# A decoder block with a product-key expert mixer: first-table products in halves between the groups of the gate build, and gate stores issued by ScalarE

## The chip, the cores and the metric

The kernel runs on one core of a Trainium2 chip. The core has five engines that run side by side, each with its own queue of instructions in a fixed order: TensorE (PE, matrix products), VectorE (DVE, elementwise work), ScalarE (ACT, activations and copies), GpSimd (POOL) and SyncE (SP, here only an issuer of transfers). Matrix products write to PSUM, everything else lies in SBUF or in device memory, and transfers (DMAs) move data between the two. The metric is the device time of one execution in microseconds (us). "Start us, us" in a row of the timeline are the start, counted from the first instruction, and the duration.

## The reference

A sequence of 512 tokens with 1024 features goes through one layer: a mixer (state-space heads beside latent attention), a norm, then an expert mixer (PEER), and a norm. Only the expert mixer matters here:

```python
def block(xb):
    q = (xb @ w_query).reshape(T, PEER_HEADS, 2, PEER_HALF_DIM)
    s = jnp.einsum('thkd,hknd->thkn', q, sub_keys)
    sv, si = lax.top_k(s, K)
    ...
    top_s, top_pos = lax.top_k(cand_s, K)
    expert_idx = jnp.take_along_axis(cand_i, top_pos, axis=-1)
    gate = jax.nn.softmax(top_s, axis=-1)
    u = jnp.take(u_table, expert_idx, axis=0)
    act = jax.nn.gelu(jnp.einsum('td,thkd->thk', xb, u), approximate=False)
    v = jnp.take(v_table, expert_idx, axis=0)
    return jnp.einsum('thk,thkd->td', gate * act, v)
```

Each token picks 8 x 16 = 128 of 16384 experts, each an (i, j) pair of 128 x 128 keys. For each one the token's product with a row of the U table goes through a Gelu, is weighted by the gate and multiplies a row of the V table.

## The kernel before

The kernel does not gather these rows for most tokens. For 384 columns (tokens of blocks 0 to 2, of which the last 16 are treated apart, so NU = 368) it multiplies densely with all 16384 experts: 128 *U products* (128 experts each) give Gelu values for all tokens, a *gate matrix* that is zero except for the chosen experts multiplies them, and 128 *V products* accumulate the output. The fourth block of 128 tokens is gathered row by row with indirect transfers during the V phase.

Precision: each fp32 weight tile is split into a high part (`wih`, ScalarE, L109, a copy to a narrower format) and a low part (`wil`, VectorE, L119, the difference), and each product is made of three matmuls (`mm3`, L71): high by high, high by low, low by high. The class `Stream` (L80) does this for all weights in one list of items: `get(n)` issues the low part of item n+2, the high part of item n+3 and the load of item n+5 (`wir`, L91, on SP's queue), so that PE finds its weights ready. `item()` takes the next one.

One U product (`u_chunk`, L1221) takes one item, makes 8 x 3 matmuls into a PSUM tile `pu` (two buffers), fills 16 columns with ones (L1229) and writes the Gelu of the rest to `act` (L1230). 54 of the products (LEAD) are made ahead of the V phase, the others inside it, one beside each V product. Where the 54 are made is decided when the program is written out, by `drive` (L1270): it keeps two counters of estimated time, `tm[0]` for PE and `tm[1]` for VectorE, and lets a step of U (4.07 on the first counter, and 1.2 on the second, for the low part) go before the next piece of VectorE work as long as `tm[0] <= tm[1]`. Up to 43 products fit until a second pool opens, then 52. The pieces come from generators: the index decoding (`stage2`) and then the gate build (`build_g`, L1126).

The gate build has 48 groups of 8 tokens, 16 to a block. For each, VectorE makes one-hot rows from the indices (`hot`: `ij` at L1134, `g` at L1139, one group ahead of PE), PE multiplies them (16 small matmuls, L1157 and L1158, into two `pw` tiles; `pw` has four buffers), and ScalarE copies the result to a staging tile `stg` (L1160, two copies). A staging tile holds four groups. There are two of them, in turn. When one is full, it is stored to device memory in two parts, `gs0` (128 KB, L1164) and `gsp` (1920 KB, L1165), both issued on SP's queue. Two generators put further pieces between the groups: 16 row products (`ug_dots`) in groups 1 to 16, and a few small steps (`ug_head`) in groups 30 to 38. `g_head` transposes the next block's indices on PE (L1115).

Behind the build, `load_g` (L1321) reads the first two pieces of the gate matrix back from `gs0` into `gt` (L1325, SP's queue), the U products still missing from the 54 are made, and the V phase begins: `P` (L1348) is the product of `act` and `gt`, `Ph` and `Pl` (L1361, L1368) are its high and low part, and 18 matmuls (L1377, L1378, L1381) add it to the output accumulators `va`.

Of the kernel before, what the change touches and what calls it, by code (L numbers as in the profile page):

```python
# [17 lines left out]
AF = mybir.ActivationFunctionType  # L18
# [14 lines left out]
NU = NT - UG  # L33
LEAD = 54
KEEP = 43
RES = 2
LASTC = 120
T_U = 4.07
# [15 lines left out]
def tile_block(ctx: ExitStack, tc: tile.TileContext, I, out):  # L54
    nc = tc.nc
    ctx.enter_context(tc.manual_schedule())
    V, A, T, G = nc.vector, nc.scalar, nc.tensor, nc.gpsimd
# [3 lines left out]
    def pool(name, bufs=1, **kw):  # L61
        p = tc.alloc_tile_pool(name=name, bufs=bufs, **kw)
        opened.append(p)
        return p
# [6 lines left out]
    def mm3(ps, lh, ll, rh, rl, start, stop):  # L71
        T.matmul(ps, lh, rh, start=start, stop=False)  # L72
        T.matmul(ps, lh, rl, start=False, stop=False)  # L73
        T.matmul(ps, ll, rh, start=False, stop=stop)  # L74

    def chain(*gs):
        for g in gs:
            yield from g
# [115 lines left out]
    gs0 = dram.tile([NT // 32, 128, 8, 32], F32, name="gs0")  # L194
    gsp = dram.tile([NT // 32, 128, 120, 32], F32, name="gsp")
# [29 lines left out]
    lo_on = [V]  # L225
# [17 lines left out]
    def item():  # L243
        cnt[0] += 1
        return win.get(cnt[0] - 1)
# [86 lines left out]
    def proj(i):  # L332
        if i < 2:
            return two[i]
        hl = item()
        ps = pa()
        for k in range(8):
            proj_k(ps, hl, k)
        return ps
# [226 lines left out]
    for i in range(13):  # L566
        ps = proj(i)
# [63 lines left out]
    for i in range(13, 18):  # L631
        ps = proj(i)
# [13 lines left out]
    for n in range(8):  # L646
# [3 lines left out]
        h, l = item()  # L650
        for kk in range(2):
            k = kp * 2 + kk
# [33 lines left out]
    pu = lambda: psU.tile([128, 512], F32, name="pu")  # L686
# [35 lines left out]
    def v_proj(p):  # L722
        wh, wl = item()
        vh = ml.tile([128, NB, 256], F32R, name="vh", bufs=2)
        vl = ml.tile([128, NB, 256], F32R, name="vl", bufs=2)
        vv[p] = (vh, vl)
        for b2 in range(2):
            ps = pp()
            for e in range(2):
                b = b2 * 2 + e  # L730
                bs = slice(b * 128, (b + 1) * 128)
                for k in range(2):
                    ks = slice(k * 256, k * 256 + 256)
                    mm3(ps[:, e * 256:(e + 1) * 256], kvh[:, k, bs], kvl[:, k, bs], wh[:, ks], wl[:, ks],
                        k == 0, k == 1)
            evac(ps, vh[:, b2 * 2:b2 * 2 + 2].rearrange("p a b -> p (a b)"),
                 vl[:, b2 * 2:b2 * 2 + 2].rearrange("p a b -> p (a b)"))
            yield

    def qk_nope(h):  # L740
        wh, wl = item()
        ps = pp()
        for k in range(3):
            ks = slice(k * 128, k * 128 + 128)
            mm3(ps, wh[:, ks], wl[:, ks], qlh[:, k], qll[:, k], k == 0, k == 2)
        QN[h] = pair("qn")
        A.activation(QN[h][0], ps, AF.Copy, scale=SCALE)
        V.scalar_tensor_tensor(QN[h][1], ps, SCALE, QN[h][0], op0=OP.mult, op1=OP.subtract)
        yield
        ps = pp()  # L750
        for k in range(2):
            ks = slice(384 + k * 128, 512 + k * 128)
            mm3(ps, wh[:, ks], wl[:, ks], kvh[:, k], kvl[:, k], k == 0, k == 1)
        KN[h] = pair("kn")
        evac(ps, *KN[h])
        yield
# [72 lines left out]
    g = chain(qk_nope(1), v_proj(0))  # L829
# [3 lines left out]
    for st in range(39):  # L833
        h, q = divmod(st, 4)
        if q == 0 and h:
            g = iter(())
            if h < 7:
                g = chain(qk_nope(h + 1), v_proj(h // 2)) if h % 2 == 0 else chain(q_pe(h // 2 + 1), qk_nope(h + 1))
# [39 lines left out]
    XTH = xt.tile([128, 8, S], F32R, name="XTH")  # L878
    XTL = xt.tile([128, 8, S], F32R, name="XTL")
    one = xt.tile([128, UG], F32, name="one")  # L880
# [245 lines left out]
    def build_g():  # L1126
        jij = gb.tile([128, 3, 4, 128, 2], F16, name="ij")

        def hot(n):
            ijT, gT = GT[n // 16]  # L1130
            r = n % 2
            col = ijT[:, n % 16 // 2, r].rearrange("p e (q c) -> p (e q) c", c=2)
            b2 = [128, 8, 128, 2]
            V.tensor_tensor(jij[:, 1 - r:3 - r].rearrange("p e q i c -> p (e q) i c"), iotaE[:, None].to_broadcast(b2),  # L1134
                            col[:, :, None, :].to_broadcast(b2), op=OP.is_equal)
            g = gb.tile([128, 2, 4, 128, 2], F16, name="g", bufs=2)
            b4 = [128, 2, 4, 128, 2]
            gv = gT[:, n % 16].rearrange("p e (q c) -> p e q c", c=2)
            V.tensor_tensor(g, jij[:, 1][:, None].to_broadcast(b4), gv[:, :, :, None, :].to_broadcast(b4), op=OP.mult)  # L1139
            return jij[:, 2 - 2 * r], g[:, 0], g[:, 1]  # L1140

        nxt = hot(0)
        dots, head = ug_dots(), ug_head()
        tm[1] += 3.0
        yield 2.6
        for n in range(48):
            b, g = divmod(n, 16)
            oj, oi, g1 = nxt
            if n < 47:
                nxt = hot(n + 1)  # L1150
            if g % 4 == 0:
                stg = gs[n // 4 % 2].tile([128, 128, 32], F32, name="stg")
            for hf in range(2):
                ps = pw()
                for t in range(4):
                    q, c = hf * 2 + t // 2, t % 2
                    T.matmul(ps[:, t * 128:(t + 1) * 128], oj[:, q, :, c], oi[:, q, :, c], start=True, stop=False)  # L1157
                    T.matmul(ps[:, t * 128:(t + 1) * 128], oj[:, q, :, c], g1[:, q, :, c], start=False, stop=True)  # L1158
                q0 = g % 4 * 8 + hf * 4
                A.activation(stg[:, :, q0:q0 + 4],  # L1160
                             ps.rearrange("p (t i) -> p i t", t=4), AF.Copy, scale=1.0 / GSC)
            tm[0] += 1.1
            if g % 4 == 3:
                nc.sync.dma_start(gs0[b * 4 + g // 4], stg[:, 0:8])  # L1164
                nc.sync.dma_start(gsp[b * 4 + g // 4], stg[:, 8:])  # L1165
            if g == 12 and b < 2:
                g_head(b + 1)
            if n >= 1:
                tm[1] += next(dots, 0.0)
            if n in (30, 32, 34, 36, 38):  # L1170
                tm[1] += next(head)
            yield 2.42 if n < 47 else 0.1
# [39 lines left out]
    aps = [pool("act")]  # L1212
    an = [0]
    ACT = {}

    def act_tile():
        k = an[0] % LEAD >= KEEP
        an[0] += 1
        return aps[k].tile([128, NT], F32, name="act", bufs=LEAD - KEEP if k else KEEP)

    def u_chunk(c, psum=None):  # L1221
        h, l = item()
        h = h.rearrange("p (k j) -> p k j", k=8)
        l = l.rearrange("p (k j) -> p k j", k=8)
        ps = (psum or pu)()[:, :NU]
        for k in range(8):
            mm3(ps, h[:, k], l[:, k], XTH[:, k, :NU], XTL[:, k, :NU], k == 0, k == 7)
        ACT[c] = act_tile()
        A.activation(ACT[c][:, NU:], one, AF.Copy)  # L1229
        A.activation(ACT[c][:, :NU], ps, AF.Gelu)  # L1230

    u_chunk(0, pw)
    win.la = 1
# [25 lines left out]
    tm = [0.0, 0.0]  # L1259

    def step_u():
        un[0] += 1
        u_chunk(un[0] - 1)
        tm[0] += T_U
        if lo_on[0] is V:
            tm[1] += 1.2

    un = [uc]

    def drive(fill):  # L1270
        while True:
            if tm[0] <= tm[1] and un[0] < (LEAD - RES if len(aps) > 1 else KEEP):
                step_u()
                continue
            c = next(fill, None)
            if c is None:
                return
            tm[1] += c

    fill = iter(())  # L1280
    for m in range(17):
        if m == 16:
            step_u()
        w_query_fm(m)
        lo_on[0] = G
        tm[0] += T_Q
        if m:
            fill = chain(fill, stage1(m - 1))
            tm[1] = max(tm[1], tm[0] - 3.0)
        while tm[1] < tm[0] + T_Q:  # L1290
            c = next(fill, None)
            if c is None:
                break
            tm[1] += c
# [18 lines left out]
    UR["hd"] = gb.tile([128, UG], F32, name="uhd")  # L1313
    UR["w"] = gb.tile([UG, 128], F32, name="uw")
    UR["m"] = gb.tile([UG, 2], F32, name="um")
    drive(build_g())
    close(gb, *gs)
    vst = pool("vst")
    gt = {}
# [1 line left out]
    def load_g(q):  # L1321
        if q < 32 and q not in gt:
            gt[q] = vst.tile([128, NT // 32, 4, 32], F32, name="gt", bufs=2)
            src, q0 = (gs0, q * 4) if q < 2 else (gsp, q * 4 - 8)
            nc.sync.dma_start(gt[q], src[:, :, q0:q0 + 4, :].rearrange("b j i t -> j b i t"))  # L1325

    for q in range(2):
        load_g(q)
    uc = un[0]
    while uc < LEAD:  # L1330
        u_chunk(uc)
# [118 lines left out]
    fill = gather()  # L1450
# [174 lines left out]
```

## Time and profile before

| | |
|---|---|
| median of three runs | 1623.73 us (1623.13 to 1624.22) |
| profiled execution, its time | 1623.08 us |
| its span, first to last instruction | 1621.3 us |
| PE busy | 1581.0 us, 98% |
| DVE busy | 1357.4 us, 84% |
| ACT busy | 708.1 us, 44% |
| POOL busy | 481.4 us, 30% |
| mean granted TensorE clock | 0.998 |
| first and last copy of the gate build (L1160) | 594.8 and 765.9 us |
| transfers | 395.42 MB, mean 244 GB/s |

Busy shares are averages over stages that have different limits, so the stretch of the gate build, some 590 to 770 us, is read by itself, in windows and in the timelines of single engines. In a row of the timeline, "x1" is the number of instructions merged, and the bracket gives the idle time of the engine before it and what ended it. In a row of a tile or line stand minimum, median and maximum in ns. In a window row each engine's busy time stands with its count of instructions, then the granted clock, the share of the transfer engines that was busy, and GB/s. In the list of waits stand the total in us, the number of times and the longest. PE's matmuls are pipelined: a row's duration is longer than its distance to the next.

### The profile page before, as it was taken

What the parts mean: (1) busy time and instruction counts of PE and PEld (TensorE: products, weight loads), DVE (VectorE), ACT (ScalarE), POOL (GpSimd) and SP (SyncE); (2) the same over time, 40 slices, a digit from 0 to 9 for tenths busy, and PEclk for the clock granted to TensorE, in tenths of its full rate; (3) what the DMA queues carried; (4) which work ended last, traced back from release to release, by engine and by line L of the source; (5) the groups of instructions that cost most, each with busy time, mean ns of one, the idle gap of its engine ahead of it and who ended that gap; (6) DMA issues with size and microseconds to landing.
All of it is one profiled execution on the core that took longest, in us unless ns stands there. A gap on an engine that the chain in (4) does not pass through costs nothing.

```text
span 1621.3 us, 23808 instructions
## 1 busy us (share of the span) xinstructions
PE 1581.0 (98%) x8643; PEld 1393.0 (86%) x8643; DVE 1357.4 (84%) x2564; ACT 708.1 (44%) x1231; POOL 481.4 (30%) x340
## 2 busy tenths in 40 slices
PE   6999999999999999999999999999999999999997
PEld 5777878888888999999999999999999999888886
DVE  8978667747799999998478888888888888889877
ACT  5575467641433445555433433333333333333341
POOL 0000010000133223100035555555555555555300
PEclk9999999999999999999999999999999999999999
DMA  6242122364432459767689999999999999999973
GB/s 243 94 157 91 46 77 57 114 235 143 133 92 81 136 179 344 272 241 255 201 282 360 358 341 342 359 352 343 349 351 350 343 343 360 353 338 362 334 226 118
DMA packets 152253, 395.42 MB, mean 244 GB/s; under 512 B 12776, under 2 KB 65720, under 8 KB 150344
## 3 DMA queue, kind: packets, MB, share of 16 engines
q1 hardware_dynamic: 108408, 238.35, 43.3%
q0 software_dynamic: 43584, 155.29, 26.1%
q8 instruction: 68, 1.11, 0.3%
q14 instruction: 49, 0.40, 0.1%
q10 hardware_dynamic: 144, 0.26, 0.0%
HBM read 359.99 MB, written 31.78 MB: 242 GB/s over the span
## 4 chain that ended last, share of the span: by engine, by line
PE 74%; DVE 18%; ACT 3%; issue 3%; DMA 2%; SPq 0%; DVEq 0%; ACTq 0%
PE va L1377 10%; PE va L1381 10%; PE va L1378 10%; PE pu L72 9%; PE pu L74 8%; PE pu L73 8%; PE pa L74 3%; PE pa L73 3%; PE pa L72 3%; DVE ij L1134 2%; DVE wil L119 2%; DVE t L955 1%; DMA wir<-ut 1%; DVE ti L959 1%; DVE ti L952 1%
## 5 line engine op out<-in xcount | busy, mean ns | idle before, releaser
L109 ACT ACTIVATE wih<-wir 128x1024 fp32r<-128x1024 f32 (+2 forms) x269 | 278.0, 1034 | 275.0 <-DMA wir<-v 94.4
L119 DVE TENSOR_TENSOR wil<-wir,wih 128x1024 fp32r<-128x1024 f32 (+1 forms) x254 | 301.9, 1189 | 98.7 <-ACT wih L109 53.8
L74 PE MATMUL pu<-XTH,wil 128*128 128x368 f32 x1008 | 331.8, 329 | 1.0 <-DVE wil L119 0.9
L72 PE MATMUL pu<-XTH,wih 128*128 128x368 f32 x904 | 299.0, 331 | 1.3 <-ACT act L1230 1.3
L73 PE MATMUL pu<-XTL,wih 128*128 128x368 f32 x904 | 296.9, 328 | 0.0
L1378 PE MATMUL va<-wil,Ph 128*128 128x512 f32 x726 | 282.7, 389 | 0.0
L1415 POOL DMA_INDIRECT row<-u,ix x128 | 190.9, 1491 | 256.7 <-DVE row L1426 126.1
L1415 POOL DMA_INDIRECT row<-v,ix x128 | 193.8, 1514 | 168.5 <-DVE ac L1432 142.9
L74 PEld LDWEIGHTS pu<-XTH,wil 128*128 128x128 f32 x1008 | 189.1, 188 | 1.7 <-DVE wil L119 1.6
L72 PEld LDWEIGHTS pu<-XTH,wih 128*128 128x128 f32 x904 | 169.5, 188 | 4.8 <-ACT act L1230 1.9
L73 PEld LDWEIGHTS pu<-XTL,wih 128*128 128x128 f32 x904 | 169.8, 188 | 2.9
L1377 PE MATMUL va<-wih,Ph 128*128 128x512 f32 x432 | 168.6, 390 | 0.0
L1432 DVE SCALAR_TENSOR_TENSOR ac<-row,hd,ac 128x1024 f32<-128x1024 f32 x128 | 164.0, 1281 | 3.5 <-DMA row<-v,ix 1.2
L1378 PEld LDWEIGHTS va<-wil,Ph 128*128 128x128 f32 x726 | 136.3, 188 | 25.8
L1230 ACT ACTIVATE act<-pu 128x368 f32<-128x368 f32 x126 | 59.9, 476 | 219.5 <-PE pu L74 219.4
L1426 DVE SCALAR_TENSOR_TENSOR row<-row,x 128x1024 f32<-128x1024 f32 x128 | 150.3, 1219 | 3.9 <-DMA row<-u,ix 3.7
L109 ACT ACTIVATE wihx<-wir 128x1024 fp32r<-128x1024 f32 x67 | 71.1, 1061 | 146.1 <-DMA wir<-v 120.5
L1381 PE MATMUL va<-wih,Pl 128*128 128x512 f32 x432 | 133.3, 390 | 0.0
L119 DVE TENSOR_TENSOR wil<-wir,wihx 128x1024 fp32r<-128x1024 f32 x62 | 75.8, 1223 | 51.4 <-issue 36.8
L1377 PE MATMUL va<-wihx,Ph 128*128 128x512 f32 x294 | 114.9, 391 | 0.0
L1381 PEld LDWEIGHTS va<-wih,Pl 128*128 128x128 f32 x432 | 81.0, 188 | 17.2
L1377 PEld LDWEIGHTS va<-wih,Ph 128*128 128x128 f32 x432 | 81.2, 188 | 15.9
(458 smaller groups left out, 3066.3 us busy)
## 6 DMA issues: line engine op xcount, KB each, us to landing
wir<-ut SPq DMA_DIRECT2D x128, 512.0 KB, 5.7
wir<-v SPq DMA_DIRECT2D x128, 512.0 KB, 6.6
gsp<-stg SPq DMA_DIRECT2D x12, 1920.0 KB, 7.4
gt<-gsp SPq DMA_DIRECT2D x30, 768.0 KB, 9.9
wir<-wo SPq DMA_DIRECT2D x26, 512.0 KB, 3.6
wir<-wf SPq DMA_DIRECT2D x18, 512.0 KB, 3.3
wir<-wqr SPq DMA_DIRECT2D x16, 512.0 KB, 3.6
de<-acd POOLq DMA_DIRECT2D x8, 512.0 KB, 5.2
```

Of the source, the lines that this page charges most:

```text
L72: T.matmul(ps, lh, rh, start=start, stop=False)
L73: T.matmul(ps, lh, rl, start=False, stop=False)
L74: T.matmul(ps, ll, rh, start=False, stop=stop)
L109: A.activation(h, r, AF.Copy)
L119: self.lo(n).tensor_tensor(l, r, h, op=OP.subtract)
L1230: A.activation(ACT[c][:, :NU], ps, AF.Gelu)
L1377: T.matmul(va[b][e], Ph[:, bs], h[:, cs], start=c == 0, stop=False)
L1378: T.matmul(va[b][e], Ph[:, bs], l[:, cs], start=False, stop=False)
L1381: T.matmul(va[b][e], Pl[:, bs], h[:, cs], start=False, stop=c == 127)
L1415: G.indirect_dma_start(out=R[s], out_offset=None, in_=I["u"] if s < 128 else I["v"], in_offset=bass.IndirectOffsetOnAxis(ap=ix[:, s % 128: ...
L1426: V.scalar_tensor_tensor(r, r, 1.0, x3, op0=OP.mult, op1=OP.mult, accum_out=hd[:, s:s + 1])
L1432: V.scalar_tensor_tensor(ac, r, hd[:, s - 128:s - 127], ac, op0=OP.mult, op1=OP.add)
```

## The change

A U product is now issued in two halves of 12 matmuls by `u_half`. The first takes the item and the PSUM tile, and the second ends with the two activations. `UO` holds a product of which one half is issued. `drive` counts T_U / 2 for each half and has a second argument: at least that many halves before each further piece. It is 1 for the gate build and 0 elsewhere. A group counts 0.95 in place of 1.1 on the first counter. If a half is pending at the end of the build, its second half follows behind `load_g`. The two stores of a staging tile are issued by ScalarE, in its own queue, in place of SP.

```diff
-            tm[0] += 1.1
+            tm[0] += 0.95
             if g % 4 == 3:
-                nc.sync.dma_start(gs0[b * 4 + g // 4], stg[:, 0:8])
-                nc.sync.dma_start(gsp[b * 4 + g // 4], stg[:, 8:])
+                nc.scalar.dma_start(gs0[b * 4 + g // 4], stg[:, 0:8])
+                nc.scalar.dma_start(gsp[b * 4 + g // 4], stg[:, 8:])
...
+    UO = {}
+
+    def u_half(c, e, psum=None):
+        if e == 0:
+            UO[c] = [z.rearrange("p (k j) -> p k j", k=8) for z in item()] + [(psum or pu)()[:, :NU]]
+        h, l, ps = UO[c]
+        for k in range(4 * e, 4 * e + 4):
+            mm3(ps, h[:, k], l[:, k], XTH[:, k, :NU], XTL[:, k, :NU], k == 0, k == 7)
+        if e:
+            del UO[c]
+            ACT[c] = act_tile()
+            A.activation(ACT[c][:, NU:], one, AF.Copy)
+            A.activation(ACT[c][:, :NU], ps, AF.Gelu)
+
     def u_chunk(c, psum=None):
-        h, l = item()
...
-        A.activation(ACT[c][:, :NU], ps, AF.Gelu)
+        for e in range(2):
+            u_half(c, e, psum)
...
     def step_u():
-        un[0] += 1
-        u_chunk(un[0] - 1)
-        tm[0] += T_U
-        if lo_on[0] is V:
+        e = len(UO)
+        u_half(un[0], e)
+        un[0] += e
+        tm[0] += T_U / 2
+        if not e and lo_on[0] is V:
             tm[1] += 1.2
...
-    def drive(fill):
+    def drive(fill, least=0):
+        n = 0
         while True:
-            if tm[0] <= tm[1] and un[0] < (LEAD - RES if len(aps) > 1 else KEEP):
+            if (tm[0] <= tm[1] or n < least) and un[0] < (LEAD - RES if len(aps) > 1 else KEEP):
                 step_u()
+                n += 1
                 continue
             c = next(fill, None)
             if c is None:
                 return
             tm[1] += c
+            n = 0
...
         if m == 16:
             step_u()
+            step_u()
...
-    drive(build_g())
+    drive(build_g(), 1)
...
     for q in range(2):
         load_g(q)
+    if UO:
+        step_u()
     uc = un[0]
```

More of the change, by code (lines that the diff above doesn't have):

```diff
@@ L1219, in act_tile @@
         return aps[k].tile([128, NT], F32, name="act", bufs=LEAD - KEEP if k else KEEP)
-    def u_chunk(c, psum=None):
-        h, l = item()
[L1223 to L1230, printed above, removed]
+    UO = {}
[10 more added lines that the diff above has]
+            A.activation(ACT[c][:, :NU], ps, AF.Gelu)
+    def u_chunk(c, psum=None):
+        for e in range(2):
+            u_half(c, e, psum)
     u_chunk(0, pw)
```

## The prediction

> **What bounds the kernel now.** I read the page first: busy shares and the slices.
>
> ```profile
> PE 1581.0 (98%) x8643; PEld 1393.0 (86%) x8643; DVE 1357.4 (84%) x2564; ACT 708.1 (44%) x1231; POOL 481.4 (30%) x340
> PEclk9999999999999999999999999999999999999999
> ```
>
> TensorE (PE) bounds the whole at an undisturbed clock, so only its idle time can be won. The second view is the busy time by stages: the stretch that the change touches, and the V phase behind it.
>
> ```profile
> core 0: us, PE busy (x) PEld busy (x) DVE busy (x) ACT busy (x) POOL busy (x), PEclk, DMA share, GB/s
> 590.82:795.74 204.92, 198.12 (x1665) 190.81 (x1665) 178.91 (x179) 110.73 (x218) 23.48 (x16) 1.00 0.74 260
> 795.74:1000.00 204.26, 204.26 (x1058) 185.72 (x1057) 166.57 (x250) 81.10 (x133) 97.71 (x66) 1.00 0.92 324
> 1000.00:1200.00 200.00, 200.00 (x1039) 182.15 (x1038) 168.06 (x242) 74.41 (x123) 111.14 (x75) 1.00 0.96 349
> ```
>
> In the V phase PE is busy in every microsecond. In the first stretch it idles 204.92 - 198.12 = 6.8 us. Its matmul ends are modelled and cover the start of each gap, so I count the idle time a second way, with ScalarE's timeline. The Gelu of a U product (L1230) starts when its 24 matmuls end.
>
> ```profile
> 590.34 0.48 ACT L1230 ACTIVATE act<-pu 128x368 f32<-128x368 f32 x1 [0.68 <-PE pu L74]
> 594.34 0.48 ACT L1230 ACTIVATE act<-pu 128x368 f32<-128x368 f32 x1 [1.66 <-PE pu L74]
> 601.22 0.48 ACT L1230 ACTIVATE act<-pu 128x368 f32<-128x368 f32 x1 [2.38 <-PE pu L74]
> 606.20 0.48 ACT L1230 ACTIVATE act<-pu 128x368 f32<-128x368 f32 x1 [2.38 <-PE pu L74]
> 692.75 0.48 ACT L1230 ACTIVATE act<-pu 128x368 f32<-128x368 f32 x1 [2.39 <-PE pu L74]
> 701.46 0.48 ACT L1230 ACTIVATE act<-pu 128x368 f32<-128x368 f32 x1 [2.39 <-PE pu L74]
> 764.90 0.48 ACT L1230 ACTIVATE act<-pu 128x368 f32<-128x368 f32 x1 [2.38 <-PE pu L74]
> 773.89 0.48 ACT L1230 ACTIVATE act<-pu 128x368 f32<-128x368 f32 x1 [2.47 <-PE pu L74]
> 787.26 0.48 ACT L1230 ACTIVATE act<-pu 128x368 f32<-128x368 f32 x1 [1.91 <-PE pu L74]
> 795.26 0.48 ACT L1230 ACTIVATE act<-pu 128x368 f32<-128x368 f32 x1 [0.44 <-PE pu L74]
> L1230 ACT ACTIVATE act<-pu x38: 457/478/481, 590.3 to 795.3; 128x368 f32<-128x368 f32 x38
> L1115 PE MATMUL px<-ident,ijg 128*128 128x128 f32 x8 | 1.2, 273 | 0.0
> ```
>
> The first two Gelus are U17 and U18 with nothing between: a U costs PE 4.00 us. From 601.22 to 606.20 lie one group and one U: 4.98, so a group costs 0.985 (taken so from several such steps), the changeover on both sides included. From U17 to U54 are 37 U products, all 48 groups and two sets of transposes: 37 x 4.00 + 48 x 0.985 + 1.2 = 196.5 us of work in 795.26 - 590.34 = 204.9. So PE idles **8.4 us** there. It is spread: 601.22 - 594.34 = 6.88 for two groups and one U (5.97), 0.9 idle; 701.46 - 692.75 = 8.71 for three groups and one U (6.96), 1.75 idle, and once more so near 755; 787.26 - 773.89 = 13.37 for three U, 1.37 idle; the rest in bits.
>
> Why it idles in the build is read from VectorE's (DVE) timeline, the first four rows, and from the list of waits (total, times, longest).
>
> ```profile
> 690.02 1.22 DVE L119 TENSOR_TENSOR wil<-wir,wih 128x1024 fp32r<-128x1024 f32 x1
> 691.15 1.22 DVE L1134 TENSOR_TENSOR ij<-iotaE,ijT 128x2048 f16<-128x2048 f16 x1
> 696.32 1.23 DVE L1134 TENSOR_TENSOR ij<-iotaE,ijT 128x2048 f16<-128x2048 f16 x1
> 761.03 1.22 DVE L1139 TENSOR_TENSOR g<-ij,gT 128x2048 f16<-128x2048 f16 x1
> PE pw L1157 <- DVE g L1139: 4.1, 4, 1.5
> ACT wih L109 <- DMA wir<-ut: 8.0, 2, 7.0
> PE pu L72 <- ACT act L1230: 1.1, 1, 1.1
> ```
>
> From 691.15 to 696.32 DVE prepares two groups without a pause: 2.585 each when adjacent; a split (wil) of a U adds 1.13 to 1.14. Where groups come without U between, PE (0.985 a group) starves behind DVE (2.585).
>
> **The change part by part.** *Where the U products go.* I walk the two counters of drive. Before, they place U17 to U47 before the build ends (31), with runs of two or three groups bare, and U48 to U53 behind it. With halves, 0.95 a group, and at least one half before each further group, they give U17 to U49 and the first half of U50: 33.5. No two groups are adjacent any more; groups 0, 1 and 18 on get mostly one half each, a few get two, groups 2 to 7 a whole U as before. All 54 lead products still precede the V phase, so no work is added on PE except changeovers: 48 groups now stand singly, and 48 x 0.985 charges each with both sides already. PE's floor for the stretch stays 196.5 us: the last lead product U53 and U54 end at 590.34 + 196.5 = 786.8 against 795.26.
>
> *Does DVE keep up?* Its last group is ready at 761.03 + 1.22 = 762.25. Before that it did the splits of U17 to U46; in the new order those of U47 to U49 come too: 3 x 1.14 = 3.4, so 765.7, less about 1.0 that it waited for PE before (below nothing it cannot cost: the splits must be done). PE, never idle, would reach group 47 after U18 to U49 and 47 groups: 590.34 + 32 x 4.00 + 47 x 0.985 + 1.2 = 765.8. The two bounds meet. Neither has slack, and each has to wait for the other now and then: group n+2's one-hot writes the buffer that group n's matmuls read. I charge this coupling 0.8 us; its ends are 0 and the 4.1 us that PE waits for g now. Group 47 then ends at 766.6 + 1.0 = 767.6, and U50 to U54 follow, 5 x 4.00: 787.6.
>
> *Halves.* A half keeps its PSUM tile across a group. pu has two buffers and pw four, so no group is refused a tile: nothing. The split, high part and load of a U are issued with its first half, in the old order; the Gelu up to a group (3 us) later; U53's Gelu is needed far later, as the V phase takes products from 0 on: nothing.
>
> *Stores on ScalarE's queue.* The rows are, in this order: issues and copies by tile and by line, the longest work of ScalarE in a U from the page, SP's waits, SP's timeline at the end of the build, three steps of the V phase's start, and the DMA issues with the time to landing.
>
> ```profile
> L1165 SPq DMA_DIRECT2D gsp<-stg x12: 413/426/937, 608.2 to 766.9; - x12
> L1160 ACT ACTIVATE stg<-pw x96: 592/597/622, 594.8 to 765.9; 128x512 f32<-128x512 f32 x96
> L1528 ACTq DMA_DIRECT2D out_dram<-xr x1: 369/369/369, 1617.9 to 1617.9; - x1
> L91 SPq DMA_DIRECT2D wir<-ut x9: 328/332/4300, 742.5 to 797.1; - x9
> L109 ACT ACTIVATE wih<-wir 128x1024 fp32r<-128x1024 f32 (+2 forms) x269 | 278.0, 1034 | 275.0 <-DMA wir<-v 94.4
> SPq L1164 <- ACT stg L1160: 36.0, 12, 4.5
> 766.49 0.33 SPq L1164 DMA_DIRECT2D gs<-stg  x1
> 768.39 3.44 SPq L1325 DMA_DIRECT2D gt<-gs  x2
> 771.89 4.78 SPq L91 DMA_DIRECT2D wir<-ut  x2
> 788.47 0.55 DVE L1348 TENSOR_TENSOR P<-act,gt 128x384 f32<-128x384 f32 x1
> 791.64 0.52 ACT L1361 ACTIVATE Ph<-P 128x384 fp32r<-128x384 f32 x1
> 792.19 0.56 DVE L1368 TENSOR_TENSOR Pl<-P,Ph 128x384 fp32r<-128x384 f32 x1 [3.17 <-ACT Ph L1361]
> gt<-gs SPq DMA_DIRECT2D x2, 768.0 KB, 10.1
> gsp<-stg SPq DMA_DIRECT2D x12, 1920.0 KB, 7.4
> wir<-ut SPq DMA_DIRECT2D x32, 512.0 KB, 3.8
> ```
>
> SP loses 12 pairs of issues and the 36 us that it stood waiting for stg with loads behind it. ScalarE gains 12 x (0.33 + 0.43) = 9 us of issue, behind its own stg copies, so the wait is short. Behind a pair are queued the high part (wih) of a U three ahead, the next Gelu and the next copies. In the late build a block of four groups and two U takes PE at least 4 x 0.985 + 2 x 4.00 = 11.9 us; of that ScalarE works 8 x 0.60 (copies) + 2 x (1.03 + 0.48) = 7.8, so a hold below 4.1 us a block delays nobody. One ACT-queue issue in the trace took 0.37 us; the dearest issue on SP, behind a full queue, 4.3. I take 0.8 a pair, near the first, since ScalarE's queue holds nothing else: nothing on the path. Ends: 0, and 4.3 + 0.3 = 4.6 a pair, which is 0.5 over the slack in each of the eight late blocks: 4 us.
>
> *The stall after the build.* The load at 771.89 stood behind the last stores and two gt loads and held a wih for 7 us, which held U50's Gelu and cost PE the 1.37. In the new order three more U have issued their loads before load_g, and the loads behind load_g belong to items read later, so that goes. The next thing late could be gt: issued when the first store has landed, 768.39 - 766.49 = 1.9 after it, and landing 10.1 later. New: group 47 at 767.6, copies 1.1, so 768.7 + 1.9 + 10.1 = 780.7, and three short steps (P, Ph, Pl, 0.55 + 0.52 + 0.56, with their handovers under 3 us) to the first V matmul: 784 against 787.6. Hidden by 4 us; without that cover each microsecond more is one on the path.
>
> [...]
>
> *Sum.* 787.6 - 795.26 = **-7.7 us**. The V phase is the same program and PE-bound, so it moves whole. I charge 0.4 for anything that catches up there (0 to 2). -7.3 on the profiled execution's 1623.08 (its span 1621.3 and 1.8 around it) is 1615.8; that execution lies 0.65 under the median of the runs, and half of that gives 1616.1.
>
> **The rivals.** *DVE takes the path.* If DVE and PE, both without slack, trip each other more, by the upper end of the coupling (4.1) instead of 0.8, the gain falls to 4.0: about 1619.4. For it: DVE is 179 of 205 us busy in the stretch and gets 3 splits more. Against: the dots end at group 16, and DVE there runs ahead.
>
> *No gain.* The idle time only moves: into the start of the V phase (gt costs from a landing 14 us after its issue on, and all of the gain at 21) or into ScalarE holds. Then 1621 to 1625, taken as 1623.
>
> *Slower: ScalarE is held at the store.* If a store issue blocks ScalarE for longer than 4.1 us a block, copies and Gelus slip, pu's two tiles run out and PE stops. At 6.5 us a block the 8 late blocks lose 8 x 2.4 = 19 us, less 7.3: 1635. It decides from 4.1 + 7.3 / 8 = 5.0 us. For it: the 4.3 us issue on SP. Against: that one came behind 1.9 MB of store and two gt loads on one queue; on ScalarE's queue a store meets nothing of its own.
>
> *Slower: stores land late.* Stores now compete with loads in place of going ahead of them. Block n+2's copies reuse block n's stg. A store needs 7.4 us, two U loads of a block 2 x 3.8: 15.0 at worst, where a block, about 12, is allowed; then 8 x 3 = 24 us of ScalarE wait, of which its slack of 4.1 a block takes all. At 17 us of landing the wait is 5 a block, past the slack by 0.9, and 8 x 0.9 = 7 us takes the gain; at 18.5 it is 6.5 a block and 1635, as above. [...]
>
> **How the numbers follow.** Forecast 0.62 (1614 to 1617.5); DVE on the path 0.14; no gain 0.13; ScalarE held 0.07; stores late 0.04. A difference under 0.2% (3.2 us) can't be told from none: the first two are faster, 0.76; the third the same, 0.13; the last two slower, 0.11. The range begins at PE's floor with nothing charged (8.4 less than 1623.08 is 1614.7) less 1.5 for an overestimated group cost, 1613.2, and reaches past the DVE rival to 1620.9.
>
> **What would show it.** In the changed profile the first V matmul stands at 787 to 788; PE idles some 1 to 2 us from U17 to there; no gap of 1.7 is left between groups; ScalarE's queue shows 24 issues of about 0.4 us. Wrong would be: PE waiting for g by 4 us and more (DVE), P waiting for gt (read-back), or stg copies waiting for a store.

## The result, and the profile after

The changed kernel takes 1617.48 us (median of six runs, 1616.28 to 1619.66) against 1623.97 us (six runs) before: a ratio of 0.9958 with a 95% interval of 0.9948 to 0.9969, so 6.5 us less (5.0 to 8.4). The forecast was 1616.1 in a range of 1613.2 to 1620.9.

The profiled execution took 1618.11 us, its span 1616.4 us. PE's granted clock fell to half for 3.4 us near 265 us in it, far ahead of the changed code. The profile of before has no such fall, and U18's Gelu comes 1.4 us earlier there. So the stretch of the change is compared by itself, from the Gelu of U18 (594.34 us before, 595.71 after) to the first V matmul. The two windows, the first of the kernel before, the second of the changed one:

```profile
594.34:795.10 200.76, 193.96 (x1642) 186.91 (x1640) 174.75 (x175) 109.09 (x214) 23.48 (x16) 1.00 0.75 264
```

```profile
595.71:790.00 194.29, 193.12 (x1641) 185.73 (x1639) 173.52 (x173) 108.41 (x211) 23.54 (x16) 1.00 0.77 271
```

6.5 us went, and by the window PE's idle time fell from 6.80 to 1.17 us. Busy time fell by only 0.8, since no work was taken away. From the first V matmul to the end of the span it is 1621.3 - 795.1 = 826.2 before and 1616.4 - 790.0 = 826.4 after: the V phase moved whole.

Three rows of the list of waits of the changed kernel, over the build (total, times, longest):

```profile
PE pw L1157 <- DVE g L1139: 1.2, 3, 0.5
DVE gT L1123 <- ACT gT L1122: 3.7, 2, 2.2
ACT act L1232 <- issue: 2.2, 1, 2.2
```

The first row is the wait for one-hot rows, down from 4.1. The second was 1.1 before (longest 0.8), and the third is new. Their longest waits belong together, and ScalarE's timeline shows where:

```profile
707.32 1.80 ACTq L1165 DMA_DIRECT2D gsp<-stg  x1
709.16 0.22 ACT L1232 ACTIVATE act<-one 128x16 f32<-128x16 f32 x1 [2.24 <-issue]
709.64 1.08 ACT L1160 ACTIVATE stg<-pw 128x512 f32<-128x512 f32 x2
710.60 0.46 ACT L1121 ACTIVATE ijT<-px 128x128 f16<-128x128 f32 x2
```

One issue of a store took 1.80 us instead of 0.45. Behind it stood the copies of the next block's indices, VectorE waited 2.2 us for them, and then PE for VectorE, 0.4 and 0.5 us at two of the next groups. In the late build two groups and one U now follow each other like this, first two Gelus of the kernel before, then three of the changed one:

```profile
680.52 0.48 ACT L1230 ACTIVATE act<-pu 128x368 f32<-128x368 f32 x1 [2.39 <-PE pu L74]
686.64 0.48 ACT L1230 ACTIVATE act<-pu 128x368 f32<-128x368 f32 x1 [2.39 <-PE pu L74]
```

```profile
739.21 0.48 ACT L1233 ACTIVATE act<-pu 128x368 f32<-128x368 f32 x1 [1.55 <-PE pu L74]
745.21 0.48 ACT L1233 ACTIVATE act<-pu 128x368 f32<-128x368 f32 x1 [1.33 <-PE pu L74]
751.21 0.48 ACT L1233 ACTIVATE act<-pu 128x368 f32<-128x368 f32 x1 [1.33 <-PE pu L74]
```

6.00 us a step, where two adjacent groups and a U took 6.12. The runs of three groups and a U, 8.71 for 6.96 of work, no longer occur.

### The profile page after: what moved, and what is told of

It reads as the page before. It is cut to its first block, busy times and chain, and to the rows that moved or that the text cites. A ratio compares the mean times of both kernels' runs of the same rounds, so it can differ in the third digit from the quotient of the medians.

```text
span 1616.4 us, 23785 instructions
## 1 busy us (share of the span) xinstructions
PE 1581.7 (98%) x8643; PEld 1392.5 (86%) x8643; DVE 1357.5 (84%) x2564; ACT 708.9 (44%) x1231; POOL 479.2 (30%) x340
## 4 chain that ended last, share of the span: by engine, by line
PE 80%; DVE 14%; ACT 3%; DMA 1%; issue 1%; DVEq 0%; ACTq 0%
PE va L1391 10%; PE va L1395 10%; PE va L1392 10%; PE pu L72 10%; PE pu L74 10%; PE pu L73 10%; PE pa L74 3%; PE pa L73 3%; PE pa L72 3%; DVE t L955 1%; PE pw L73 1%; PE pw L74 1%; PE pw L72 1%; PE pw L1157 1%; DVE wil L119 1%; PE pw L1158 1%
## 5 line engine op out<-in xcount | busy, mean ns | idle before, releaser
L119 DVE TENSOR_TENSOR wil<-wir,wih 128x1024 fp32r<-128x1024 f32 (+1 forms) x254 | 302.0, 1190 | 94.0 <-ACT wih L109 54.8
L1429 POOL DMA_INDIRECT row<-v,ix x128 | 189.2, 1478 | 173.1 <-DVE ac L1446 147.8
L119 DVE TENSOR_TENSOR wil<-wir,wihx 128x1024 fp32r<-128x1024 f32 x62 | 75.8, 1223 | 41.3 <-issue 29.9
```

The lines of the kernel that those rows point to most:

```text
L119: self.lo(n).tensor_tensor(l, r, h, op=OP.subtract)
L1429: G.indirect_dma_start(out=R[s], out_offset=None, in_=I["u"] if s < 128 else I["v"], in_offset=bass.IndirectOffsetOnAxis(ap=ix[:, s % 128: ...
```

## The experiments

Theory A: PE idled because VectorE could not supply adjacent groups, and more U products in the build fill that time. Rivals: only their number counts and not the halves (the first form of A), or only the spacing (B); the freed SP queue is what helps (C); adjacent groups wait for something of their own, not for VectorE (D). Each ratio is against the kernel before, run on the same chip in the same set. Times of different sets come from different chips, so a difference between two edited kernels of different sets is also given counted from each set's own kernel before, or by the stretch. The halves with a group still counted 1.1 were not run, so what the counter adds to them stays open.

**The changed kernel again.** No edit.

> The changed kernel again, beside the others of this set: about 6.5 us below before, near 1617.5 (both theories). In its trace U18's Gelu to the first V matmul should take about 194.3 us, as in the first profile (before: 200.8).

Measured: 1617.33 us, ratio 0.9959 (0.9945 to 0.9972). U18's Gelu to the first V matmul: 193.8 us. The long store issue is there again, 1.68 us at the same place, so it is no chance of one execution. All five runs had a mean granted clock of 0.997. In this set the fourteen runs of the kernel before with that clock have a median of 1624.43 us, so at the same clock the gain is 7.1 us.

**The counter alone.**

```diff
-            tm[0] += 1.1
+            tm[0] += 0.95
```

> Only the group's 0.95 on the planner's first counter; U products whole, stores on SP. The counters then place 33 whole U products in the build (before 31, changed kernel 33.5), two groups adjacent between most of them, never three. Theory A (what counts is how many U products lie in the build): the triples (2 x 1.75 us idle) go and the stall behind the build (1.37) goes, the pairs stay at VectorE's 6.12 per two groups instead of 5.97: 3 to 5.5 us gained, near 1619.5. Theory B (what counts is the spacing in halves): the pairs keep starving PE, at most 2 us gained, 1622 or more.

Measured: 1621.75 us, ratio 0.9989 (0.9980 to 0.9998), 2.5 us less: between the two bands. The window of the stretch in this kernel:

```profile
594.21:792.70 198.49, 193.84 (x1641) 186.82 (x1639) 173.46 (x175) 108.51 (x213) 23.54 (x16) 1.00 0.76 267
```

33 U products lie in the build, almost as many as in the changed kernel (33.5), and still it is 4.2 us behind it there. So the number alone gives less than half of the gain, under the 3 to 5.5 us of theory A's first form, and a little more than B allowed. Its pairs run at VectorE's pace:

```profile
690.26 0.48 ACT L1230 ACTIVATE act<-pu 128x368 f32<-128x368 f32 x1 [2.39 <-PE pu L74]
696.39 0.48 ACT L1230 ACTIVATE act<-pu 128x368 f32<-128x368 f32 x1 [2.39 <-PE pu L74]
```

6.13 us a step. Either VectorE is too slow for adjacent groups (A2), or these wait for their own tiles (D).

**The stores alone.**

```diff
-                nc.sync.dma_start(gs0[b * 4 + g // 4], stg[:, 0:8])
-                nc.sync.dma_start(gsp[b * 4 + g // 4], stg[:, 8:])
+                nc.scalar.dma_start(gs0[b * 4 + g // 4], stg[:, 0:8])
+                nc.scalar.dma_start(gsp[b * 4 + g // 4], stg[:, 8:])
```

> Only the two stores moved to ScalarE's queue; U products whole and counted as before. Theory A: PE's waits in the build hang on VectorE and not on a transfer, so 0 to 1.4 us gained (the stall behind the build at most), 1622.5 to 1624. Rival C (the freed SP queue is what helps): 3 us or more gained, below 1621.

Measured: 1624.99 us, ratio 1.0007 (0.9998 to 1.0016). No gain.

```profile
594.06:795.40 201.34, 194.06 (x1641) 186.87 (x1639) 175.03 (x175) 110.22 (x214) 23.53 (x16) 1.00 0.74 264
```

The stretch is no shorter (200.76 before). Rival C falls.

**The halves without the stores.** The changed kernel with the two lines above on SP again.

> The changed kernel with both stores issued by SP again. Theory A: as fast as the changed kernel within 1.5 us, or up to 1.2 us faster, since the one store issue that held ScalarE for 1.8 us ahead of the transposed indices is gone: 1616.3 to 1618. Rival C: it loses 3 us or more of the gain, 1620.5 or more.

Measured: 1617.38 us, ratio 0.9960 (0.9946 to 0.9973).

```profile
595.68:788.80 193.12, 192.83 (x1641) 185.80 (x1639) 172.96 (x172) 107.94 (x211) 23.55 (x16) 1.00 0.77 273
```

As fast as the changed kernel; in its trace 0.7 to 1.2 us shorter in the stretch, the size of the waits behind the long store issue, but the medians don't show it. The whole gain is the halves' and the planner's, none of it the stores'.

**Low parts on GpSimd.** The same edit in three kernels, meant to relieve VectorE: from group 17 to the end of the build the difference of L119 is computed by GpSimd. In the kernel before, in the one with the counter alone, and in the changed one:

```diff
-    win = Stream(..., lo=lambda n: lo_on[0])
+    win = Stream(..., lo=lambda n: G if lo_g else lo_on[0])
...
         for n in range(48):
+            if n == 17:
+                lo_g.append(1)
...
+    lo_g.clear()
     close(gb, *gs)
```

> The kernel before, same order of U products and groups, but from group 17 to the end of the build the low parts (wil) are computed by GpSimd in place of VectorE. Theory A2 (where groups stand adjacent PE waits for VectorE's one-hot rows): VectorE loses 14 x 1.14 = 16 us of work there, pairs go from 6.12 to about 5.95 and triples lose part of their 1.75: 2.5 to 4.5 us faster, near 1620.5. Rival D (adjacent groups wait for something of their own, their PSUM tiles or ScalarE's copies): no change, within 1 us.

> The kernel with 0.95 on the planner's counter alone (whole U products, pairs of groups; 1621.75 by itself), with the low parts from group 17 on by GpSimd. Theory A2: the pairs no longer wait, 15 x 0.15 to 0.2 plus the 1.1 at groups 18 and 19: 3 to 4 us faster than without, near 1618, as fast as halves or nearly. Rival D: 1621 to 1622 as before.

> The changed kernel with the low parts from group 17 on by GpSimd. Theory A2: its late build is at PE's own pace already (5.98 to 6.00 for two groups and a U) and only 1.2 us of waits for VectorE are left, so 0 to 1.5 us faster: 1616 to 1617.3. If VectorE set the pace (the forecast's first rival), more: 1615 or less.

Measured: 1652.92 (ratio 1.0169, 1.0153 to 1.0185), 1646.08 (1.0131, 1.0115 to 1.0148) and 1632.28 us (1.0046, 1.0031 to 1.0060). All three are slower than the kernel before, by 29, 22 and 8 us, against every expectation. Against the same kernels without the edit they lose 29, 24 and 15 us, each counted from the kernel before of its set. In the first two PE's granted clock also fell: to 0.89 from 675 to 770 us in the first, and to 0.989 and 0.990 in the mean of the two profiled executions, where the third had 0.998. So a part of their loss is the clock's. In the third it stayed at 1.00 from 590 to 820 us. VectorE's and GpSimd's timelines in the last one show where the time goes:

```profile
697.93 3.31 DVE L1140 TENSOR_TENSOR g<-ij,gT 128x2048 f16<-128x2048 f16 x1
701.34 1.23 DVE L1135 TENSOR_TENSOR ij<-iotaE,ijT 128x2048 f16<-128x2048 f16 x1
702.60 1.23 DVE L1140 TENSOR_TENSOR g<-ij,gT 128x2048 f16<-128x2048 f16 x1
```

```profile
697.42 2.74 POOL L119 TENSOR_TENSOR wil<-wir,wih 128x1024 fp32r<-128x1024 f32 x1 [4.53 <-PE pu L74]
704.68 2.74 POOL L119 TENSOR_TENSOR wil<-wir,wih 128x1024 fp32r<-128x1024 f32 x1 [4.53 <-PE pu L74]
```

A `g` that starts 0.5 us into GpSimd's subtraction takes 3.31 us instead of 1.23: it ends 1.08 us after GpSimd does, as if it had run only then. VectorE is spared 1.14 us a U and loses 2.08. From 675 to 800 us the 29 `g` took 2.23 us in the mean and the 28 `ij` 1.37, beside 13 subtractions of 2.82. Why a `g` there lasts past GpSimd's end isn't shown. As an experiment on theory A2 these runs don't count as meant. They do show that VectorE's time decides: made longer, it costs PE, which waits 14.3 us for one-hot rows in the third. The kernel with singly placed groups loses least (15 against 29).

**The transposed indices two groups earlier**, in the changed kernel:

```diff
-            if g == 12 and b < 2:
+            if g == 10 and b < 2:
```

> The changed kernel with the transposed indices of the next block made two groups earlier (behind group 10 in place of 12), so that ScalarE's three small copies for them no longer stand right behind a store issue. If the 1.8 us store issue ahead of them is what made VectorE wait 2.2 us and PE 1.2 us, those two waits go: 0.5 to 1.5 us faster than the changed kernel, 1616 to 1617. If it was only a chance of that execution: no difference.

Measured: 1617.28 us, ratio 0.9950 (0.9936 to 0.9964); the changed kernel stood at 1617.33 and 1617.48. The issues of the large store, first in the changed kernel run again, then in this one:

```profile
L1165 ACTq DMA_DIRECT2D gsp<-stg x12: 326/450/1675, 609.2 to 771.2; - x12
```

```profile
L1165 ACTq DMA_DIRECT2D gsp<-stg x12: 356/450/681, 608.6 to 770.0; - x12
```

The long issue is gone, and the stretch took 193.1 us instead of 193.8. The edit moved only the copies, yet the issue itself became short too, so this run doesn't tell the copies' place from the issue's length. What makes that one issue long stays open. The worth of both, under 1 us, can't be told in the times.

**Low parts left out, with the counter alone.** No other engine works beside VectorE here: from group 17 to the end of the build the third matmul of a U takes the high part once more. The kernel leaves out a part of the U products' precision by this and serves as a measurement only.

```diff
-                l = self.tiles(n, 1)[:, :r.shape[-1]]
-                self.lo(n).tensor_tensor(l, r, h, op=OP.subtract)
+                if lo_g:
+                    l = h
+                else:
+                    l = self.tiles(n, 1)[:, :r.shape[-1]]
+                    self.lo(n).tensor_tensor(l, r, h, op=OP.subtract)
```

> The kernel with 0.95 on the planner's counter alone (whole U products, pairs of groups; 1621.75), and from group 17 to the end of the build the low parts are left out: the third matmul takes the high part instead, so PE's work is the same and VectorE has 16 x 1.14 us less, with no other engine working beside it. It leaves out a part of the U products' precision. Theory A2 (adjacent groups wait for VectorE): pairs go from 6.12 to 5.92, so 15 x 0.2 and about 1 us at groups 18 and 19: near 1617.7, as fast as with halves. Rival D (adjacent groups wait for their PSUM tiles, ScalarE's copies or a changeover): 1621 to 1622.

Measured: 1618.74 us, ratio 0.9965 (0.9951 to 0.9979), 3.0 us less than with the low parts (3.5 counted from each set's own kernel before); the stretch is 3.3 us shorter, and its pairs have dropped from 6.13 to 5.93 us:

```profile
595.55:790.70 195.15, 192.31 (x1642) 187.12 (x1640) 157.05 (x159) 107.52 (x213) 23.53 (x16) 1.00 0.75 272
```

```profile
691.19 0.48 ACT L1236 ACTIVATE act<-pu 128x368 f32<-128x368 f32 x1 [2.29 <-PE pu L74]
697.12 0.48 ACT L1236 ACTIVATE act<-pu 128x368 f32<-128x368 f32 x1 [2.33 <-PE pu L74]
```

This is A2: adjacent groups wait for VectorE, and with VectorE relieved they cost PE 5.93, less than two single groups with their changeovers (6.00). Rival D falls.

**Low parts left out, in the changed kernel.** The same edit, and the same part left out.

> The changed kernel with the same low parts left out. Theory A2: PE stands at its own pace already and only some 0.5 to 1.2 us of waits for VectorE can go: 1616 to 1617.3. If VectorE sets the pace in the changed kernel: 1615 or less.

Measured: 1615.08 us, ratio 0.9944 (0.9931 to 0.9958), 2.3 us below the changed kernel (2.7 counted from each set's own kernel before). By the time alone that is next to the rival's band (1615 or less) and below theory A2's. But the clock has a part in it: all five runs had a mean granted clock of 0.998, and the changed kernel 0.997 in all five of its second set; its only run at 0.998 took 1616.28. The trace is free of this:

```profile
594.10:786.70 192.60, 192.60 (x1642) 185.72 (x1640) 155.04 (x157) 109.63 (x213) 23.86 (x16) 1.00 0.77 273
```

The stretch took 192.6 us, 1.2 to 1.7 less than in the changed kernel (193.8 and 194.3), and PE was busy in all of it: 18 us less VectorE work buy 1.2 to 1.7 us. So in the changed kernel VectorE costs PE only its last waits. 192.6 is also PE's floor, measured.

**The large store in twelve pieces**, in the changed kernel, to lengthen ScalarE's hold:

```diff
-                nc.scalar.dma_start(gsp[b * 4 + g // 4], stg[:, 8:])
+                for z in range(8, 128, 10):
+                    nc.scalar.dma_start(gsp[b * 4 + g // 4][:, z - 8:z - 8 + 10], stg[:, z:z + 10])
```

> The changed kernel with each large store of the gate matrix cut in 12 pieces, all issued by ScalarE: 13 issues a block of some 0.35 to 0.45 us, about 5 us, where the forecast counts 4.1 us of slack a block. By the forecast's slack: 8 late blocks x about 1 us, 5 to 11 us slower than the changed kernel, 1622 to 1628. If issues cost ScalarE less than their rows show, or PE's spare tiles take the hold: within 1.5 us of the changed kernel, below 1619.

Measured: 1659.02 us, ratio 1.0215 (1.0201 to 1.0228), 41.7 us more than the changed kernel. The issues cost more than a piece's row of 0.45 suggested:

```profile
692.80 0.33 ACTq L1164 DMA_DIRECT2D gs<-stg  x1
693.16 6.82 ACTq L1166 DMA_DIRECT2D gsp<-stg  x12
700.03 1.06 ACT L109 ACTIVATE wih<-wir 128x1024 fp32r<-128x1024 f32 x1 [7.26 <-DMA gsp<-stg]
```

In this block ScalarE stands for 7.3 us. In the first six blocks, up to 715 us, the two stores hold it for 6.7 to 9.6 us, 8.1 in the mean. The kernel loses 41.7 / 12 = 3.5 us a block, but its mean granted clock was 0.991, against 0.997 in the changed kernel: some 10 us of the loss (an estimate, 0.009 x 1658.6 - 0.003 x 1616.4 of the two spans) are the clock's, which leaves some 32, 2.6 a block. A mean hold of 8.1 less the forecast's slack of 4.1 would be 4.0. So a hold above the slack does cost PE, and the slack was of the right order, if rather too small. With one large store (0.33 + 0.45 us) the hold stays far under it, which fits that the stores cost nothing.

**Without the minimum of one half**, in the changed kernel:

```diff
-    drive(build_g(), 1)
+    drive(build_g())
```

> The changed kernel without the minimum of one half between two groups (halves, 0.95 and ScalarE's stores stay). The counters then leave groups adjacent at 0 and 1, 22 and 23, 24 and 25, 26 and 27, 28 and 29, 33 and 34, with a whole U behind each. Theory A2: some 0.5 us for the first and 0.15 to 0.6 for each other, 1 to 2.5 us slower than the changed kernel: 1618.3 to 1620. If the halves alone do it: as the changed kernel, 1617.4.

Measured: 1620.90 us, ratio 0.9977 (0.9968 to 0.9986): 3.5 us worse than the changed kernel, more than expected.

```profile
596.04:793.40 197.36, 193.52 (x1642) 186.39 (x1640) 174.66 (x175) 109.58 (x213) 23.25 (x16) 1.00 0.75 269
```

```profile
596.04 0.48 ACT L1233 ACTIVATE act<-pu 128x368 f32<-128x368 f32 x1 [1.83 <-PE pu L74]
603.38 0.48 ACT L1233 ACTIVATE act<-pu 128x368 f32<-128x368 f32 x1 [2.36 <-PE pu L74]
779.65 0.48 ACT L1233 ACTIVATE act<-pu 128x368 f32<-128x368 f32 x1 [2.47 <-PE pu L74]
787.68 1.06 ACT L109 ACTIVATE wihx<-wir 128x1024 fp32r<-128x1024 f32 x1 [7.55 <-DMA wir<-v]
788.75 0.46 ACT L1233 ACTIVATE act<-pu 128x368 f32<-128x368 f32 x1
```

The first pair, groups 0 and 1, costs 603.38 - 596.04 - 5.97 = 1.4 us; PE waited for one-hot rows twice in this kernel, 1.3 and 0.6 us. The rest is the stall behind the build, which is back: the high part waits 7.55 us for its load and holds the Gelu behind it, and from U51's Gelu at 779.65 to the first V matmul at 793.4 PE needs three U (12.0) and takes 13.75. The kernel with the counter alone has the same stall (1.7 us). In both the build ends with a whole U, 50 in all; in the changed kernel with the first half of the next, whose step issues one more load ahead of `load_g`.

## Why the prediction was right

*Where PE idles, and why.* Right. PE's floor for the stretch was put at 196.5 us from U17 on, so 192.5 from U18 on; the run without low parts had PE busy in every microsecond of 192.6. That VectorE starves adjacent groups is shown by leaving its low parts out: 6.13 to 5.93 a pair.

*The stretch.* 7.7 us were forecast, 6.5 came in the first profile and 6.9 in the second (200.76 - 193.82). The term that was too small is the coupling of PE and VectorE: 0.8 charged, 1.2 to 1.7 measured above the floor of 192.6. Its cause was not the buffers of the one-hot rows, as the step had it (VectorE waited 0.3 us for PE to free one in the whole build), but mostly the store issue that held ScalarE: with SP's stores 0.5 is left. The median of 1617.48 lies at the upper end of the forecast's own band, 1614 to 1617.5.

*DVE keeps up.* Right: its pace of 6.12 for two groups and a U is slower than PE's 6.00, but with single groups it can use the lead that it gained by group 17. Two low parts of the changed kernel, with two groups between them, show the pace:

```profile
740.57 1.22 DVE L119 TENSOR_TENSOR wil<-wir,wihx 128x1024 fp32r<-128x1024 f32 x1
746.69 1.22 DVE L119 TENSOR_TENSOR wil<-wir,wih 128x1024 fp32r<-128x1024 f32 x1
```

By the two timelines the rows of group 17 are ready 3.2 us before PE uses them, those of group 47 only 0.4 us. The lead lasts just to the end of this build, so a longer one would have run at VectorE's pace (an estimate from these two leads; no run shows it). The first rival (VectorE on the path) is refuted by the run without low parts: 18 us less work gave 1.2 to 1.7.

*Halves cost nothing.* Right: 6.00 a step against the 5.97 counted.

*Stores on ScalarE cost nothing.* In the time, yes: alone (a ratio of 1.0007) and undone (1617.38 us beside the changed kernel's 1617.33) they make no measurable difference. In the trace one issue out of twelve took 1.7 to 1.8 us, where 0.8 for a pair was taken, and it stood ahead of copies on which VectorE waits. The rival "ScalarE is held" is a real mechanism; twelve pieces made it cost 41.7 us, the lower clock included.

*The stall after the build goes.* Right, and for the reason given, loads issued ahead of `load_g`, but closer than the forecast told: three more U were credited. The kernels whose build ends with a whole U have two more U in it than before, and keep 1.7 us or so of the stall; so it hangs on the last half and its one load.

*gt is hidden.* Hidden, but not by 4 us. The read-back was issued 775.4 - 770.8 = 4.6 us after the first store, where 1.9 was counted, since SP waited longer for that store to land, 4.4 us after its issue instead of 1.7:

```profile
SPq L1337 <- DMA gs<-stg: 4.2, 1, 4.2
```

P did not wait for gt, but Ph stood on ScalarE behind a high part that waited 4.9 us for its load, and was ready at 789.5, with the first V matmul at 790.0. PE lost nothing there, with little to spare. In the kernel with halves and SP's stores this row is 0.3 us, in the one with the stores alone 4.4, so the longer landing came with ScalarE's queue.

*The V phase moves whole*, with 0.4 charged: 826.2 to 826.4, so 0.2.

*Stores late.* The large store landed after 7.9 us instead of 7.4 (at most 10.8), the small one after 2.6 instead of 1.7; the 15 of the rival did not occur.

## What to carry to other kernels

Here two engines each had just enough time, and what decided was how evenly the one's work was laid between the deliveries of the other: almost the same number of products gave 2.5 us in whole pieces, and 6.5 in halves with one between any two deliveries. Read the pace of each engine for one step from its own timeline, take the sum of PE's work as the floor, and don't hope for more. Moving transfers to another engine's queue gained nothing here (1.0007), where no wait of PE in the build ended with them, and it put the issues in front of that engine's own work (one of 1.80 us).

## What was unexpected of the hardware

A VectorE instruction beside a GpSimd subtraction took 3.31 us in place of 1.23, and moving 14 or so such subtractions to the idle engine made each kernel 15 to 29 us slower than without.

PE's granted clock fell near 265 us in nine of the fourteen profiles, with halves and with whole U products alike, at two short gaps of PE (1.53 and 0.44 us in the changed kernel). Windows of the changed kernel (first) and of the one before, in its profile without the fall:

```profile
262.00:266.00 4.00, 2.07 (x7) 1.58 (x8) 2.46 (x7) 2.04 (x6) 0.00 (x0) 0.78 0.02 4
266.00:270.00 4.00, 4.00 (x22) 3.43 (x21) 2.56 (x6) 2.35 (x8) 0.00 (x0) 0.79 0.17 50
```

```profile
262.00:266.00 4.00, 2.06 (x10) 1.61 (x11) 2.46 (x7) 2.04 (x6) 0.00 (x0) 1.00 0.01 4
266.00:270.00 4.00, 4.00 (x25) 3.47 (x24) 2.66 (x7) 3.23 (x10) 0.00 (x0) 1.00 0.19 53
```

The program is the same there and PE is as idle in both. The 0.78 and 0.79 are means: in windows of a quarter of a microsecond the clock of the changed kernel is 0.50 from 264.3 to 267.7 us and 1.00 around it. The mean from 258 to 274 us is 0.89 in all nine profiles and 1.00 in the other five, and one fall to 0.50 of 3.4 us gives 0.89. By the windows of 4 us it begins near 265.6 in the changed kernel run again (0.95, then 0.63) and near 264.8 in the one with SP's stores (0.85, then 0.72), both estimates. Where U18's Gelu was read, it stands at 594.1 to 594.3 us without the fall (four profiles) and at 595.5 to 596.3 with it (seven), so the fall costs some 1.6 us. The times show it too: in the set of the second run of the changed kernel, the kernel before has a median of 1622.85 us in its seven runs at a mean clock of 0.998 and of 1624.43 in the fourteen at 0.997.

PE was busy in 2.07 of the 4 us in which the fall begins and in 2.06 where none came, and no run here moved the gaps, so what triggers it stays open.
